# Weight sums of three square products made early and kept in DRAM, with three smaller edits, in a one-layer streaming encoder

## The chip, the core and the metric

The kernel runs on one core of a Trainium2 chip. The metric is the device time of one execution in microseconds (us). TensorE (PE) does the matmuls and loads their weights, VectorE (DVE), ScalarE (ACT) and GpSimd (POOL) do elementwise work, and the SyncE queue (SP) issues the DMAs, one after the other.

## What is computed

One layer over 1024 new frames of one stream and 64 frames of a running one, 1088 columns of width 1024 in all, in float32. The reference, cut to the parts that matter here:

```python
h = x + 0.5 * swiglu(rmsnorm(x, g_ffn1), w_ffn1_gu, w_ffn1_d)           # ffn1, D_FF = 2816
z = rmsnorm(h, g_mix) @ w_in                                            # projection: [u | q | k | v]
y_ssm = glu(s5(u));  y_att = diff_attn(q, k, v)                         # two head groups
h = h + concat(y_ssm, y_att) @ w_out                                    # square product "out", 1024 x 1024
mk, mv = rmsnorm(mem, g_mem) @ w_ck, rmsnorm(mem, g_mem) @ w_cv         # memory keys and values
q = rmsnorm(h, g_cross) @ w_cq                                          # square product "cq"
h = h + (softmax(q @ mk.T / 16) @ mv) @ w_co                            # square product "co"
y = rmsnorm(h + 0.5 * swiglu(rmsnorm(h, g_ffn2), ...), g_final)         # ffn2
```

## The kernel before

**Precision.** Every float32 operand is split in two parts of TensorE's reduced format, a high and a low part, and a product is three matmuls (hi·hi, hi·lo, lo·hi; `mm3`, L171, tiles 128 wide, mostly 272 columns). For a weight tile `split_into` (L147) makes the high part `wh` on ACT (L151), makes a second rounded copy `q` on ACT (L152), and subtracts on DVE (L153) to get the low part `wl`. `q` lies in PSUM in a pool that has one buffer, so the next split's copy waits until this subtraction has read it. `w_raw` loads a weight piece into one of four "wr" tiles, `half` gives one of four half-size "ws" tiles, `row` one of 36 rows; `wh` and `wl` have 7 buffers each.

**Squares.** The three 1024 x 1024 products are done as seven products of half size each, one per turn, in the order `TURNS = (0, 1, 3, 4, 5, 2, 6)`. Class `Block` loads the four quarters of a weight (`a11`, `a12`, `a21`, `a22`, four row blocks k each). `mix` (L433 to L435) makes three sums of quarters on POOL and `prepare` a fourth (L448), 16 POOL operations of 128x512 in all for a square. `prepare` also splits the weight (L446) and the data operand: L422 and L426 make the data's differences, L450 and L451 their high and low parts. `square` (L468) runs the turns: four output blocks i per turn, 24 matmuls each, then the additions to the outputs (L502); after each block the operand of the next turn is prepared.

**FFN.** Both FFNs use class `Operands`: `high` on ACT (L340), `low` (L345) on POOL for row blocks k in `LOW_G = (1, 3)` and on DVE for the others. POOL also makes the FFN's weight sums (L616 to L619) and its joins (L646, L647, L775).

**Memory.** `mem_proj` projects 256 memory rows, first with w_cv, then with w_ck (PE L1700, copies L1707), through `load_w`, which splits by `split_into`.

**Norm sums.** `Normed.finish` multiplies squared sums by a 128-wide matrix of ones (L543), five column tiles into two banks of PSUM, and copies a column of each out (L545, L547).

**Order.** The source appends generators to a background list `bg` and pumps them, but the final order on every engine is laid out by a scheduler that simulates the program; it may put an operation well ahead of its place in the source. SP issues the DMAs in one row, so a DMA that waits holds back those behind it. The stages from the span's start, in us: ffn1 to 752 (its last down block from 696), norm to 803, projection with the S5 scans 805 to 1030, GLU and attention to 1210, memory values to 1240, out to 1340, memory keys 1340 to 1382, cq to 1474, cross attention to 1540, co to 1643, norm, ffn2 to the end.

## Time and profile before

| | us |
|---|---|
| median of 3 runs (2411.47 to 2418.18) | 2415.66 |
| the profiled execution | 2410.96 |
| its span | 2409.2 |
| PE busy (94% of the span) | 2267.8 |
| DVE busy (68%) | 1646.8 |
| ACT busy (54%) | 1308.8 |
| POOL busy (46%) | 1102.1 |
| mean granted TensorE clock, of 1 | 0.978 |

The time is the span and what lies around it, 1.8 us here. PE is busy nearly throughout, so the time can fall by what PE idles in, by what it works through at a lower granted clock, or by less work for it. A granted clock of 1 is 2.4 GHz and of 0.5 is 1.2 GHz; a stretch of T us with a mean clock c has lost about T x (1 - c) if PE had work all through.

### The profile page before, as it was taken

What the parts mean: (1) busy time and instruction counts of PE and PEld (TensorE: products, weight loads), DVE (VectorE), ACT (ScalarE), POOL (GpSimd) and SP (SyncE); (2) the same over time, 40 slices, a digit from 0 to 9 for tenths busy, and PEclk for the clock granted to TensorE, in tenths of its full rate; (3) what the DMA queues carried; (4) which work ended last, traced back from release to release, by engine and by line L of the source; (5) the groups of instructions that cost most, each with busy time, mean ns of one, the idle gap of its engine ahead of it and who ended that gap; (6) DMA issues with size and microseconds to landing.
All of it is one profiled execution on the core that took longest, in us unless ns stands there. A gap on an engine that the chain in (4) does not pass through costs nothing. (4 is left out here: it accounts for less than half of the span.)

```text
span 2409.2 us, 44963 instructions
## 1 busy us (share of the span) xinstructions
PE 2267.8 (94%) x16914; PEld 2199.7 (91%) x16914; DVE 1646.8 (68%) x3296; ACT 1308.8 (54%) x2538; POOL 1102.1 (46%) x846
## 2 busy tenths in 40 slices
PE   6899999999999999989999899898899999998998
PEld 6899999998999998978889898798899999998997
DVE  6557543358899594269968688787654454479897
ACT  6554544546545422267856667576555544464543
POOL 2666777744144400035444510455776666644350
PEclk8999999999999999999999999999999999999999
DMA  6232444443412446333443411133232222262312
GB/s 207 75 114 82 118 110 118 117 174 141 145 42 82 155 126 171 93 128 105 134 156 111 164 50 53 54 116 94 83 97 81 78 70 77 81 227 82 110 47 93
DMA packets 267237, 262.61 MB, mean 109 GB/s; under 512 B 36446, under 2 KB 216715, under 8 KB 267019
## 3 DMA queue, kind: packets, MB, share of 16 engines
q1 hardware_dynamic: 266928, 259.72, 33.7%
q8 instruction: 133, 2.18, 0.4%
q14 instruction: 86, 0.70, 0.1%
q10 hardware_dynamic: 90, 0.02, 0.0%
HBM read 186.51 MB, written 68.58 MB: 106 GB/s over the span
## 5 line engine op out<-in xcount | busy, mean ns | idle before, releaser
L171 PE MATMUL b<-r,wh 128*128 128x272 f32 (+4 forms) x9600 | 1684.7, 296 | 54.1 <-DVE r L724 21.5
L171 PEld LDWEIGHTS b<-r,wh 128*128 128x128 f32 x9600 | 1420.1, 191 | 72.3 <-DVE r L724 26.2
L171 PE MATMUL b<-r,wl 128*128 128x272 f32 (+4 forms) x4800 | 1053.1, 295 | 25.4 <-DVE wl L153 25.2
L171 PEld LDWEIGHTS b<-r,wl 128*128 128x128 f32 x4800 | 782.7, 190 | 29.6 <-DVE wl L153 29.4
L596 DVE TENSOR_TENSOR r<-b,r 128x272 f32<-128x272 f32 x440 | 172.1, 434 | 247.1 <-PE b L171 227.7
L153 DVE TENSOR_TENSOR wl<-wr,q 128x512 fp32r<-128x512 f32 x304 | 207.2, 682 | 182.0 <-issue 94.6
L151 ACT CAST wh<-wr 128x512 fp32r<-128x512 f32 x304 | 187.7, 621 | 252.0 <-PE b L171 226.4
L152 ACT CAST q<-wr 128x512 fp32r<-128x512 f32 x304 | 179.9, 592 | 246.7 <-DVE wl L153 244.5
L451 DVE TENSOR_TENSOR r<-r,r 128x544 fp32r<-128x544 f32 x224 | 213.0, 968 | 24.1 <-ACT r L450 22.9
L433 POOL TENSOR_TENSOR ws<-r,r 128x512 f32<-128x512 f32 x32 | 53.2, 1670 | 307.9 <-DVE ws L1826 125.2
L153 DVE TENSOR_TENSOR wl<-ws,q 128x512 fp32r<-128x512 f32 x158 | 107.7, 681 | 96.2 <-PE b L171 53.4
L151 ACT CAST wh<-ws 128x512 fp32r<-128x512 f32 x158 | 98.0, 620 | 137.3 <-PE b L171 112.1
L152 ACT CAST q<-r 128x512 fp32r<-128x512 f32 x146 | 86.3, 591 | 125.5 <-DVE wl L153 125.3
L450 ACT CAST r<-r 128x544 fp32r<-128x544 f32 x224 | 143.5, 649 | 8.8 <-DMA r<-hid_d 7.2
L724 DVE SCALAR_TENSOR_TENSOR r<-b,r 128x272 f32<-128x272 f32 (+4 forms) x328 | 132.3, 438 | 22.7 <-PE b L171 21.7
L152 ACT CAST q<-ws 128x512 fp32r<-128x512 f32 x158 | 93.8, 594 | 87.4 <-DVE wl L153 80.2
L646 POOL TENSOR_TENSOR r<-r,r 128x544 f32<-128x544 f32 x44 | 61.5, 1398 | 169.8 <-DVE r L596 133.1
L153 DVE TENSOR_TENSOR wl<-r,q 128x512 fp32r<-128x512 f32 x146 | 99.5, 681 | 36.9 <-ACT q L152 35.8
L1425 POOL CAST r<-r 64x256 fp32r<-64x256 f32 x32 | 14.5, 454 | 237.2 <-ACT r L1342 221.5
L659 POOL TENSOR_TENSOR r<-r,r 128x1088 f32<-128x1088 f32 x44 | 112.0, 2548 | 8.8 <-ACT r L658 8.8
L151 ACT CAST wh<-r 128x512 fp32r<-128x512 f32 x146 | 90.0, 620 | 42.4 <-PE b L171 28.1
L137 PE MATMUL b<-ident,r 128*128 128x128 f32 (+4 forms) x649 | 92.3, 280 | 18.4 <-DMA r<-x_prompt 9.6
(343 smaller groups left out, 2965.4 us busy)
## 6 DMA issues: line engine op xcount, KB each, us to landing
wr<-w_ffn_gu SPq DMA_DIRECT2D x194, 256.0 KB, 2.9
hid_d<-r SPq DMA_DIRECT2D x44, 544.0 KB, 3.1
r<-hid_d SPq DMA_DIRECT2D x44, 544.0 KB, 6.6
h_d<-r SPq DMA_DIRECT2D x48, 272.0 KB, 2.5
r<-h_d SPq DMA_DIRECT2D x48, 272.0 KB, 2.8
r<-w_ffn_d SPq DMA_DIRECT2D x24, 512.0 KB, 7.0
wr<-w_in SPq DMA_DIRECT2D x32, 256.0 KB, 2.6
wr<-w_ffn_d SPq DMA_DIRECT2D x20, 256.0 KB, 2.8
```

Source lines behind the costliest of these rows:

```text
L137: T.transpose(out, in_, ident[:n, :n])
L151: A.copy(hi, x)
L152: A.copy(r, x)
L153: V.tensor_tensor(out=lo, in0=x, in1=r.bitcast(F32), op=ALU.subtract)
L171: T.matmul(pc[:, :c1 - c0], w, x[:, c0:c1], start=(first + i == 0 and q == 0), stop=(first + i == n - 1 and q == 2))
L433: G.tensor_tensor(out=s1, in0=a21, in1=a22, op=ALU.add)
L450: A.copy(r[:, 0], v)
L451: V.tensor_tensor(out=r[:, 1], in0=v, in1=r[:, 0].bitcast(F32), op=ALU.subtract)
L596: V.tensor_tensor(out=oc, in0=pc, in1=tc_, op=ALU.add)
L646: G.tensor_tensor(out=gate[:, T2], in0=gate[:, T2], in1=up[:, T2], op=ALU.add)
L659: G.tensor_tensor(out=up, in0=up, in1=gate, op=ALU.mult)
L724: V.scalar_tensor_tensor(out=hc_, in0=pc, scalar=0.5, in1=hc_, op0=ALU.mult, op1=ALU.add)
```

## The change

1. `LOW_G` becomes empty: `low` of every row block goes to DVE.
2. `w_split` gets a flag. In `mem_proj` the copy `q` is left out, and the low part is the raw tile minus `wh`, both in SBUF.
3. A generator `weight_sums` makes the four sums for a weight ahead of its square and stores them in `sums_d` in DRAM: for each k it loads 8 pieces of 128x2x128 into the four "ws" tiles, runs 16 POOL operations of 128x128, and stores four tiles. That is 32 loads, 64 POOL operations and 16 stores for a weight. In the source, w_out's generator stands before the projection's first unit, those of w_co and then w_cq before its third key unit. `SquareBlock` takes `Block`'s place: it loads the right quarter or sum for each turn from DRAM (28 loads of 256 KB for a square) and has no POOL work. The tiles for turns 0, 3 and 6 are "ws" tiles, those for 1 and 4 "wr" tiles, the rest rows.
4. `Normed.finish` multiplies by four columns of ones in place of 128 and uses one bank.

```diff
-LOW_G = 1, 3
+LOW_G = ()
...
-    def w_split(raw):
+    def w_split(raw, staged=True):
...
+        if staged:
+            split_into(hi, lo, raw)
+        else:
+            A.copy(hi, raw)
+            V.tensor_tensor(out=lo, in0=raw, in1=hi.bitcast(F32), op=ALU.subtract)
...
+    def weight_sums(n, w, swap=False):
+        i11, i21, i12, i22 = (1, 0, 3, 2) if swap else (0, 1, 2, 3)
+        for k in range(4):
+            ts = [half([P, 4, P]) for _ in range(4)]
+            for c, t in enumerate(ts):
+                for h in range(2):
+                    wj = w[(4 * h + k) * P:(4 * h + k + 1) * P].rearrange("p (h c n) -> p h c n", h=2, c=4)
+                    load(out=t[:, 2 * h:2 * h + 2], in_=wj[:, :, c])
+            yield
+            for c, t in enumerate(ts):
+                a11, a21, a12, a22 = (t[:, i] for i in (i11, i21, i12, i22))
+                G.tensor_tensor(out=a22, in0=a21, in1=a22, op=ALU.add)
+                G.tensor_tensor(out=a21, in0=a11, in1=a21, op=ALU.subtract)
+                G.tensor_tensor(out=a11, in0=a22, in1=a11, op=ALU.subtract)
+                G.tensor_tensor(out=a12, in0=a12, in1=a11, op=ALU.subtract)
+                store(out=sums_d[n, k, c], in_=t)
+    class SquareBlock(Block):
...
+        def fetch(self, n, k):
+            if n >= 7:
+                return
+            q, g = TURNS[n], n % 3
+            if g < 2:
+                t = self.held("wr" if g else "ws", k, (lambda: wp.tile([P, 512], F32, tag="wr", name=nm("wr"), bufs=4))
+                              if g else lambda: half([P, 512]))
+            else:
+                t = self.held("w2", k // 2, lambda: row([P, 2, 512]))[:, k % 2]
+            if q in (0, 1, 5):
+                j, h = (k if q == 0 else 4 + k), (q == 5) != self.swap
+                load(out=t, in_=self.wd[j * P:(j + 1) * P, 512 * h:512 * h + 512])
+            else:
+                i = {2: 3, 3: 0, 4: 1, 6: 2}[q] ^ self.swap
+                load(out=t.rearrange("p (c n) -> p c n", c=4),
+                     in_=sums_d[self.number, k, :, :, i].rearrange("c p n -> p c n"))
+            self.raw[q, k] = t
+        def prepare(self, q, k, late=False):
...
+            self.w[q, k] = self.held.split_w(self.raw[q, k])
+            self.operand(q, k, late)
...
-            p, q = bank(), bank()
+            p = bank()
             for t, (t0, n) in enumerate(HTILES):
...
+                T.matmul(p[:n, 4 * t:4 * t + 4], self.acc[:, c, t0:t0 + n], ones[:, 0:4], start=True, stop=True)
...
+    bg.append(weight_sums(0, a["w_out"][0]))
     for f in range(4):
...
+        if hd == SUMS_AT:
+            bg.append(chain(weight_sums(2, a["w_co"][0]), weight_sums(1, a["w_cq"][0], True)))
...
-                wk = load_w(wv[:, :, c * P:(c + 1) * P])
+                wk = load_w(wv[:, :, c * P:(c + 1) * P], False)
...
-    d = Block(Held(), 4, weights_of(a["w_out"][0]), cat)
+    d = SquareBlock(0, a["w_out"][0], cat)
```

Where the scheduler puts the moved work shows in the engines' orders. First POOL at the start of ffn1's last down block (about 696 us in the trace of before), before the change; `r` are rows, L775 the down block's joins:

```order
L448 TENSOR_TENSOR r_7333<-r_7333,wr_7244 128x512
L775 TENSOR_TENSOR r_6898<-r_6898,r_6798 128x544
L775 TENSOR_TENSOR r_6900<-r_6900,r_6800 128x544
L775 TENSOR_TENSOR r_6902<-r_6902,r_6802 128x544
L775 TENSOR_TENSOR r_6904<-r_6904,r_6804 128x544
L775 TENSOR_TENSOR r_6988<-r_6988,r_6798 128x544
```

The same place after the change; L831 is the old L775, L482 to L485 are the sums of w_out in "ws" tiles:

```order
L448 TENSOR_TENSOR r_7334<-r_7334,wr_7245 128x512
L482 TENSOR_TENSOR ws_9788<-ws_9788 128x128
L483 TENSOR_TENSOR ws_9788<-ws_9788 128x128
L831 TENSOR_TENSOR r_6899<-r_6899,r_6799 128x544
L484 TENSOR_TENSOR ws_9788<-ws_9788 128x128
L485 TENSOR_TENSOR ws_9788<-ws_9788 128x128
L482 TENSOR_TENSOR ws_9789<-ws_9789 128x128
L831 TENSOR_TENSOR r_6901<-r_6901,r_6801 128x544
```

All 64 sums of w_out stand here, among the joins of the last down block, ahead of the projection; those of w_co begin behind the projection's first scans and run on into its key units, and those of w_cq follow.

Next DVE at the start of co (about 1540 us), before the change; L1866 copies the last attention output, `wl` is a low part of a weight:

```order
L451 TENSOR_TENSOR r_18299<-r_17645,r_18299 128x544
L451 TENSOR_TENSOR r_18308<-r_17662,r_18308 128x544
L422 TENSOR_TENSOR r_17645<-r_17645 128x544
L451 TENSOR_TENSOR r_18317<-r_17870,r_18317 128x544
L1866 COPY r_18254<-b_18346 128x64
L1866 COPY r_18271<-b_18346 128x64
L422 TENSOR_TENSOR r_17662<-r_17662 128x544
L451 TENSOR_TENSOR r_18326<-r_17887,r_18326 128x544
L426 TENSOR_TENSOR r_17645<-r_18095,r_17645 128x544 x2
L422 TENSOR_TENSOR r_17870<-r_17870 128x544
L426 TENSOR_TENSOR r_17662<-r_18112,r_17662 128x544 x2
L422 TENSOR_TENSOR r_17887<-r_17887 128x544
```

After the change, from the last four of the corresponding rows on (L154 is the old L153):

```order
L422 TENSOR_TENSOR r_18179<-r_18179 128x544
L426 TENSOR_TENSOR r_17971<-r_18421,r_17971 128x544 x2
L154 TENSOR_TENSOR wl_18597<-ws_18588,q_18598 128x512
L422 TENSOR_TENSOR r_18196<-r_18196 128x544
L426 TENSOR_TENSOR r_18179<-r_18563,r_18179 128x544 x2
L426 TENSOR_TENSOR r_18196<-r_18580,r_18196 128x544 x2
L154 TENSOR_TENSOR wl_18606<-ws_18590,q_18607 128x512
L154 TENSOR_TENSOR wl_18615<-ws_18592,q_18616 128x512
L154 TENSOR_TENSOR wl_18624<-ws_18594,q_18625 128x512
L154 TENSOR_TENSOR wl_18689<-wr_18632,q_18690 128x512
```

The four low parts of turn 0 stand behind the data's differences now; before the change they were made before the first of these rows, during the cross attention.

Last DVE in the memory keys' projection (about 1350 us), before the change:

```order
L153 TENSOR_TENSOR wl_16098<-wr_16095,q_16099 128x512
L451 TENSOR_TENSOR r_16286<-r_14307,r_16286 128x544
L451 TENSOR_TENSOR r_16295<-r_14308,r_16295 128x544
L422 TENSOR_TENSOR r_14307<-r_14307 128x544
L451 TENSOR_TENSOR r_16304<-r_14309,r_16304 128x544
L422 TENSOR_TENSOR r_14308<-r_14308 128x544
L451 TENSOR_TENSOR r_16313<-r_14310,r_16313 128x544
L426 TENSOR_TENSOR r_14307<-r_14311,r_14307 128x544
L153 TENSOR_TENSOR wl_16133<-wr_16130,q_16134 128x512
```

After the change (L163 is the subtraction without `q`):

```order
L163 TENSOR_TENSOR wl_16464<-wr_16461,wh_16463 128x512
L163 TENSOR_TENSOR wl_16497<-wr_16494,wh_16496 128x512
L163 TENSOR_TENSOR wl_16503<-wr_16500,wh_16502 128x512
L1763 COPY r_16210<-b_16365 128x512
L1763 COPY r_16211<-b_16371 128x512
L154 TENSOR_TENSOR wl_16592<-ws_16583,q_16593 128x512
L455 TENSOR_TENSOR r_16597<-r_14692,r_16597 128x544
```

The keys' low parts have moved ahead of cq's data operands, which stood among them.

## Rows read from the trace of the kernel before

**Rows 1.** The page, part 1: busy us of each engine, share, instructions.
```profile
PE 2267.8 (94%) x16914; PEld 2199.7 (91%) x16914; DVE 1646.8 (68%) x3296; ACT 1308.8 (54%) x2538; POOL 1102.1 (46%) x846
```

**Rows 2.** Waits of PE (us, times, longest) at 85-110, 905-920, 1240-1290, 1338-1382, 1555-1590, 1640-1662.
```profile
PE b L171 <- POOL r L345: 4.8, 3, 2.7
...
PE b L1284 <- ACT r L1286: 5.0, 1, 5.0
...
PE b L171 <- DVE r L1707: 3.9, 1, 3.9
...
PE b L1700 <- DVE wl L153: 5.1, 4, 2.3
...
PE b L171 <- DVE wl L153: 10.5, 3, 8.5
...
PE b L543 <- DVE hq L545: 3.9, 1, 3.9
```

**Rows 3.** Windows: busy time of each engine in eight stretches, granted clock (PEclk), DMA.
```profile
core 0: us, PE busy (x) PEld busy (x) DVE busy (x) ACT busy (x) POOL busy (x), PEclk, DMA share, GB/s
...
60.00:120.00 60.00, 52.64 (x376) 50.69 (x375) 34.68 (x56) 30.36 (x59) 37.57 (x27) 0.91 0.26 77
...
720.00:760.00 40.00, 35.48 (x277) 34.60 (x276) 38.66 (x56) 19.19 (x34) 24.24 (x16) 1.00 0.18 58
...
865.00:925.00 60.00, 54.44 (x345) 53.23 (x344) 57.19 (x156) 14.01 (x25) 0.00 (x0) 0.91 0.49 138
...
1242.00:1340.00 98.00, 89.47 (x678) 88.11 (x677) 80.12 (x130) 64.90 (x119) 58.39 (x40) 0.97 0.37 126
1340.00:1382.00 42.00, 33.33 (x229) 30.11 (x228) 26.84 (x42) 24.91 (x49) 16.81 (x11) 0.88 0.54 173
...
1540.00:1643.00 103.00, 90.74 (x693) 88.87 (x693) 92.75 (x148) 70.79 (x130) 60.07 (x39) 0.95 0.26 86
1643.00:1660.00 17.00, 12.27 (x76) 11.31 (x76) 15.28 (x21) 13.67 (x27) 10.10 (x7) 0.82 0.34 106
...
1740.00:2125.00 385.00, 384.86 (x3066) 384.64 (x3065) 191.47 (x333) 192.60 (x347) 251.63 (x147) 1.00 0.27 87
```

**Rows 4.** Timelines of POOL and DVE, 88-108: start, us, operation, [idle before <-releaser].
```profile
97.71 1.34 POOL L345 TENSOR_TENSOR r<-r,r 128x544 fp32r<-128x544 f32 x1
...
99.75 1.17 DVE L345 TENSOR_TENSOR r<-r,r 128x544 fp32r<-128x544 f32 x1 [3.75 <-ACT r L340]
```

**Rows 5.** Timeline of DVE at the start of out and in the memory keys.
```profile
1243.20 6.36 DVE L426 TENSOR_TENSOR r<-r,r 128x544 f32<-128x544 f32 x4
...
1253.35 0.69 DVE L153 TENSOR_TENSOR wl<-r,q 128x512 fp32r<-128x512 f32 x1 [0.66 <-ACT q L152]
...
1369.06 6.14 DVE L426 TENSOR_TENSOR r<-r,r 128x544 f32<-128x544 f32 x4
```

**Rows 6.** Timelines of PE, DVE and POOL around the start of co.
```profile
1539.81 1.01 PE L171 MATMUL b<-r,wh 128*128 128x272 f32 x6
...
1538.10 2.75 DVE L451 TENSOR_TENSOR r<-r,r 128x544 fp32r<-128x544 f32 x2 [5.56 <-ACT r L450]
...
1556.38 1.81 DVE L451 TENSOR_TENSOR r<-r,r 128x544 fp32r<-128x544 f32 x1
...
1565.59 0.71 DVE L426 TENSOR_TENSOR r<-r,r 128x544 f32<-128x544 f32 x1
1566.22 0.71 DVE L451 TENSOR_TENSOR r<-r,r 128x544 fp32r<-128x544 f32 x1
...
1557.57 1.77 POOL L434 TENSOR_TENSOR r<-wr,r 128x512 f32<-128x512 f32 x1
```

**Rows 7.** POOL by line and form: 696-760 (first row), the whole span (others).
```profile
L775 POOL TENSOR_TENSOR r<-r,r 128x544 f32<-128x544 f32 x20 | 31.3, 1571 | 32.7 <-DVE r L724 23.0 <-DVE r L775 9.4
...
L1090 POOL TENSOR_TENSOR r<-r 128x448 f32<-128x448 f32 x16 | 18.6, 1160 | 1.5 <-DVE wl L153 1.0
...
L1090 POOL TENSOR_TENSOR r<-r 128x64 f32<-128x64 f32 x8 | 2.6, 331 | 0.0
```

More of the change, by code (lines that the diff above doesn't have):

```diff
@@ L34 @@
 NPAIR = 16
+SUMS_AT = 2
 S_CHS = ((0, 360), (360, 720), (720, 1088))
@@ L153, in split_into, with load_w @@
         V.tensor_tensor(out=lo, in0=x, in1=r.bitcast(F32), op=ALU.subtract)
-    def w_split(raw):
+    def w_split(raw, staged=True):
         hi = wp.tile([P, 4, P], F32R, tag="wh", name=nm("wh"))
         lo = wp.tile([P, 4, P], F32R, tag="wl", name=nm("wl"))
-        split_into(hi, lo, raw)
+        if staged:
[3 more added lines that the diff above has]
+            V.tensor_tensor(out=lo, in0=raw, in1=hi.bitcast(F32), op=ALU.subtract)
         return hi, lo
-    def load_w(src):
-        parts = [w_split(w_raw(src[:, k:k + 4])) for k in range(0, src.shape[1], 4)]
+    def load_w(src, staged=True):
+        parts = [w_split(w_raw(src[:, k:k + 4]), staged) for k in range(0, src.shape[1], 4)]
         return [(hi[:, k], lo[:, k]) for hi, lo in parts for k in range(4)]
@@ L403, in load @@
                 self.a21[k] = held("a21", k // 2, lambda: row([P, 2, 512]))[:, k % 2]
-                halves = (wj[:, 512:1024], wj[:, 0:512]) if self.swap else (wj[:, 0:512], wj[:, 512:1024])
-                load(out=self.a11[k], in_=halves[0])
-                load(out=self.a21[k], in_=halves[1])
+                load(out=self.a11[k], in_=wj[:, 0:512])
+                load(out=self.a21[k], in_=wj[:, 512:1024])
             else:
@@ L409, in load @@
                 self.a12[k], self.a22[k] = both[:, 0], both[:, 1]
-                if self.swap:
-                    for c in range(2):
-                        load(out=both[:, c], in_=wj[:, 512 - 512 * c:1024 - 512 * c])
-                else:
-                    load(out=both, in_=wj.rearrange("p (c m) -> p c m", c=2))
+                load(out=both, in_=wj.rearrange("p (c m) -> p c m", c=2))
         def value(self, q, k, late):
@@ L448, in prepare, with operand @@
                 G.tensor_tensor(out=w, in0=w, in1=self.a11[k], op=ALU.subtract)
+            self.operand(q, k, late)
+        def operand(self, q, k, late):
+            held = self.held
             v, r = self.value(q, k, late), held("x", 4 * (held.turn[1] % 2) + k, lambda: row([P, 2, HT], F32R))
@@ L462, in product, with __init__ @@
             return p
+    sums_d = dram([3, 4, 4, P, 4, P], "sums_d")
+    def weight_sums(n, w, swap=False):
[15 more added lines that the diff above has]
+    class SquareBlock(Block):
+        def __init__(self, number, w, u, swap=False):
+            super().__init__(Held(), 4, None, u, swap=swap)
+            self.number, self.wd, self.raw = number, w, {}
+        def fetch(self, n, k):
[16 more added lines that the diff above has]
+        def prepare(self, q, k, late=False):
+            if k == 0:
+                self.held.turn[1] += 1
+            self.w[q, k] = self.held.split_w(self.raw[q, k])
+            self.operand(q, k, late)
     TURNS = (0, 1, 3, 4, 5, 2, 6)
@@ L511, in square @@
                     d.prepare(TURNS[n + 1], i, True)
+                d.fetch(n + 3, i)
                 if n in (0, 2, 3, 4):
@@ L540, in finish @@
             V.memset(ssq, 1.0)
-            p, q = bank(), bank()
+            p = bank()
             for t, (t0, n) in enumerate(HTILES):
-                T.matmul((p if t < 4 else q)[:n, (t % 4) * P:(t % 4 + 1) * P], self.acc[:, c, t0:t0 + n], ones,
-                         start=True, stop=True)
-            V.tensor_copy(ssq[:, 0:4], p.rearrange("p (t n) -> p t n", n=P)[:, :, 0])
+                T.matmul(p[:n, 4 * t:4 * t + 4], self.acc[:, c, t0:t0 + n], ones[:, 0:4], start=True, stop=True)
             n = HT - 512
-            V.tensor_copy(ssq[:n, 4:5], q[:n, 0:1])
+            V.tensor_copy(ssq[:, 0:4], p[:, 0:16].rearrange("p (t n) -> p t n", n=4)[:, :, 0])
+            V.tensor_copy(ssq[:n, 4:5], p[:n, 16:17])
             if self.rb is None:
@@ L1669, in tile_hymba_step @@
                 bg.append(subln(heads[m // 8]))
-    def weights_of(w):
-        return lambda k: w[k * P:(k + 1) * P]
     def begin(d):
-        for k in range(4):
-            d.load(1, k)
-        for k in range(4):
-            d.prepare(0, k)
-        for k in range(4):
-            d.load(3, k)
+        for n in range(3):
+            for k in range(4):
+                d.fetch(n, k)
+            if n == 0:
+                for k in range(4):
+                    d.prepare(0, k)
     h2_d = dram([KT, P, NT], "h2_d")
@@ L1815, in tile_hymba_step @@
     bg.append(cache_prep())
-    d = Block(Held(), 4, weights_of(a["w_cq"][0]), h2, swap=True)
+    d = SquareBlock(1, a["w_cq"][0], h2, swap=True)
     begin(d)
@@ L1879, in tile_hymba_step @@
         c_values(*q.popleft())
-    d = Block(Held(), 4, weights_of(a["w_co"][0]), oc)
+    d = SquareBlock(2, a["w_co"][0], oc)
     begin(d)
```

## The prediction, made before the changed kernel ran

> **What bounds the kernel now.** I read the engines' busy times first: PE is busy for 2267.8 of 2409.2 us [rows 1], so some 141 us of idle time, and what passes at half clock, are all that this change can touch, since it takes only six matmuls away. Next come the waits of PE in the stretches that the change names [rows 2], and the windows around them [rows 3]. From a window I take two losses: its length minus PE's busy time, and its length times one minus the granted clock, which is what work at the lower of the two levels (1.2 in place of 2.4 GHz) costs a PE that is busy. In 60-120 that is 7.4 + 5.4 us, in out (1242-1340) 8.5 + 2.9, in the memory keys (1340-1382) 8.7 + 5.0, in co (1540-1643) 12.3 + 5.2, in the norm behind it (1643-1660) 4.7 + 3.1: 63 us in all, the ceiling of the gain. What must not be overlooked is how close VectorE is to being a second bound: 38.7 of 40 us in 720-760 and 57.2 of 60 in 865-925.
>
> **LOW_G, start of ffn1.** PE waits 4.8 us there for three subtractions on POOL [rows 2]. Each takes 1.34 us itself and stands in a queue of weight sums and joins, while VectorE sits idle for 3.75 us ahead of its own subtraction of 1.17 us [rows 4]. Moved to VectorE (14 operations in the first 120 us, 34.7 of 60 us busy in 60-120 [rows 3]), they find room; POOL's queue shortens by as much. I take the 4.8 us and half of the clock's 5.4, minus 0.5 for subtractions that now queue behind each other: **7 us** (2 to 11). In co and the norm 8 more operations move to VectorE, at 0.63 us from start to start [rows 6], 5 us that its relief there (below) covers; without it they would cost up to those 5 us, which the lower end for co takes in.
>
> **out.** Four operations of 128x544 took 6.36 us on VectorE at 1243 [rows 5], against 0.63 us for one when POOL is idle [rows 6]: 3.8 us lost while POOL mixed weights. The copies for PE stand behind them, and PE waits 3.9 us for those [rows 2]. Without mixing that wait goes; of the other 4.6 us of idle time I count half, and of the clock's 2.9 us the same share (6.2 of 8.5): 3.9 + 2.3 + 2.1 = **8 us** (2 to 11). The 28 loads from DRAM have a whole turn or more of lead and are hidden; if they were not, each square would stall where a turn begins.
>
> **Memory keys.** Two things go. A split can start only every 1.35 us, since its copy `q` waits for the one buffer (0.69 us of subtraction and the 0.66 us of idle time in front of it [rows 5]); 16 splits take 21.6 us of a stretch of 42. Without `q` a subtraction of some 0.69 us sets the pace. And four operations took 6.14 us in place of 2.5 while POOL mixed w_cq [rows 5]; the order shows cq's operands behind the keys' low parts now. Of 8.7 us of idle time I count 6, 5.1 of it the waits for `wl` [rows 2], and the same share of the clock's 5.0, 3.4: **9 us** (4 to 13). In the memory values the PE is not kept waiting, and cq loses little as it is: nothing for either (0 to 2).
>
> **co.** From about 1554 to 1565 VectorE and POOL took turns, one operation each per 1.74 us (1.81 and 1.77 us long), where VectorE alone starts one every 0.63 us [rows 6]: seven operations took 10.9 us instead of 4.4, and PE waited 10.5 us for the low parts behind them [rows 2]. That goes. But turn 0's weights now sit in "ws" tiles, which cross attention holds almost until co's first matmul at 1539.8 [rows 6]; its low parts, earlier made during the attention, now stand in VectorE's order behind eleven operations on data and two copies. From 1538.1 on [rows 6], at 0.63 us each, I place the first at 1546.1, the others at 1549.9, 1551.3 and 1552.6, the last three 1.35 us apart by the chain of `q` [rows 5]. PE has 14, 20 and 20 matmuls of 0.125 us (385 us by 3066 [rows 3]) between them, so it waits 4.6 and 1.3 us, and in turn 1, whose fourth low part comes at 1567.0 by the same count, 1.5 us. Old losses 10.5 and 5.2 (clock), new ones 7.4, and up to 5.2 again if the clock falls: a gain of 3.1 to 8.3, **5 us** (-3 to 10).
>
> **Norm.** A narrow product saves next to nothing itself; the one bank less removes the 3.9 us wait for the copy behind VectorE's row of differences [rows 2], unless the next product, which waits for a bank as well, inherits it. Of 7.8 us I take half, **4 us** (0 to 8).
>
> **What the sums cost.** No row shows a 128x128 sum on POOL. Between 331 ns at 128x64 and 1160 ns at 128x448 [rows 7] a straight line gives 0.47 us, 30 us for a weight's 64. By the order, w_out's sums stand in ffn1's last down block, where POOL is busy for 31.3 of 64 us [rows 7]: it fits, barely, with joins of 1.57 us queued behind sums and, on SP, loads of the next stage's rows and weights behind 16 stores that wait for them. VectorE has no slack there. It has about 35 all-SBUF operations, partly slowed by the joins already; if each waits out one sum in the remaining 60% of the time, 10 us. PE was idle for 4.5 of 40 us waiting for VectorE [rows 3], so delay passes on. Between 0 and 12 I take **5 us**. Some 32 sums of w_co fall into 868-920, where POOL was empty and VectorE is full with scans: 0 to 15 us (32 by 0.47) on top of the 5.0 us wait at 912 [rows 2], **5 us** since scans with a PSUM operand or a long running time absorb most. w_cq's sums run at 955-1020 beside idle engines. Each weight costs 4.2 MB read and 4.2 written for its sums, and 7.3 MB in place of 4.2 in its square, 34 MB in all; the DMA engines are busy for 0.18 to 0.54 of the stretches concerned [rows 3]: 0 (0 to 3).
>
> **Sum.** 7 + 8 + 9 + 5 + 4 = 33 us gained, 10 lost, 23 net. Against the profiled execution, 2410.96 us, that is 2388; it lies 4.7 us under the median of the runs shown, and against that median of 2415.66 I predict **2393 us**.
>
> **Rivals.** First, *VectorE and POOL exclude each other on every sum*. In co each operation of one waited out a whole one of the other [rows 6]. If each of the 64 + 32 sums that fall into full VectorE stretches cost it 0.47 us, the bill is 45 us against 33: +12, **2428 us**. This is also how the change fails to do what it says, since w_out's sums are not made in the projection, with its idle POOL, but 100 us earlier. It turns slower from 33/96 = 0.34 us per sum, measurably from 0.42; my 10 us are 0.10. Against it: low parts that read `q` in PSUM keep 0.69 us while POOL works [rows 5], and PSUM readers are a large part of the down block. The Trainium skill, "SBUF — State Buffer" (section "SBUF: two separate sides"), calls the port pair that the two share an exclusive lock, held for a whole instruction, which a VectorE operation with two SBUF inputs meets when a GpSimd operation reads SBUF; the lockstep in co agrees, and by that rule the sums hurt just where both are full, and the keys' new subtraction without `q` would be exposed as well, were POOL not empty there now.
>
> Second, *the waits move to the next in line*. A square needs 84 us of PE (672 matmuls of 0.125 us). VectorE was busy for 92.8 us in co [rows 3]; without the 6.5 us of lockstep 86 are left, as much as PE needs. If VectorE's own sum sets the squares' pace, the keys finish early only to wait for cq's data, and the norm passes its wait on, LOW_G's 7 us alone stay against 10 lost: +3, **2419 us**, no change. For it: these 86 us. Against it: the waits stand at a few places, where a queue of data differences bunches ahead of a low part, not in every turn; PE is idle for 12.3 of the 103 us, and 10.5 of these are one bunch [rows 2, 3].
>
> Third, *everything is had*: the upper ends, 11 + 11 + 13 + 10 + 8, with no cost: -53, **2363 us**. It needs POOL's small sums to slip between VectorE's operations everywhere.
>
> **How the numbers follow.** A chance of 0.60 for the forecast, 0.15 for the lock, 0.17 for moved waits, 0.08 for everything. About 0.3%, 7 us, is what a measurement of this kernel can tell from no change. The forecast's own spread (the ends above taken as independent, some 15 us either way) crosses into no change in one case of nine, and the third rival is faster: faster 0.61, within 0.3% 0.23, slower 0.16. The range takes in the moved waits, and below, most of the forecast's spread: 2370 to 2420.
>
> **What would show it.** LOW_G: no wait of PE for a POOL subtraction before 120 us. out and keys: four data differences in 2.5 us in place of 6.4, splits in the keys less than 1.35 us apart, both windows shorter by 8 and 9 us. co: PE waits of about 5 us near 1545 in the old count and none of 8 us behind. Sums: VectorE operations in the last down block over 1.2 us long next to 0.47 us sums, and the norm beginning some 5 us late. I would be wrong most easily in the costs: if the down block ends 15 us late, the first rival is right, and if the squares still take 98 to 103 us, the second.

## The result

The changed kernel takes 2397.0 us (2393.9 to 2401.6, 4 runs) against 2415.1 us (2411.5 to 2418.2): a ratio of 0.9927, 95% interval 0.9905 to 0.9949, 18 us faster. 2393 had been forecast. A second set of runs gave 2399.2 against 2416.4. The profiled execution is one of 2398.3 us, 12.7 us below that of before, which was a quick one of its kind.

Part 1 of the page of the changed kernel, which answers to [rows 1]: PE is busy for 5 us less than before and idle for some 8 us less, so the gain is idle time and time at half clock. Its number of instructions is the same, 16914: the change takes no matmul away, where the prediction has six.

```profile
PE 2262.8 (94%) x16914; PEld 2197.2 (92%) x16914; DVE 1644.8 (69%) x3318; ACT 1290.2 (54%) x2506; POOL 1101.7 (46%) x968
```

Where it went is read best from the start of the same matmul in both traces. The first group of an S5 output unit is at 956.13 before and at 973.99 after: +17.9 us. The transposes in cq are at 1439.74 and 1434.89: -4.9. Timelines of PE, first before (L1284, L137), then after (L1340, L138):

```profile
956.13 0.39 PE L1284 MATMUL b<-r,r 128*128 128x136 f32 x2
...
1439.74 0.60 PE L137 MATMUL b<-ident,r 128*128 128x128 f32 x4
```

```profile
973.99 0.39 PE L1340 MATMUL b<-r,r 128*128 128x136 f32 x2
...
1434.89 0.60 PE L138 MATMUL b<-ident,r 128*128 128x128 f32 x4
```

The table gives such differences of starts for eight landmarks and all runs, in us against the trace of before (negative is ahead). The landmarks, named by their time before: background work in ffn1 (291), the norm's sums (803), the S5 output (956), the end of the attention (1227), late cq (1440), the end of the cross attention (1536), the norm behind co (1645), the last transposes (2397). The last columns are the median of the runs and the ratio to before with its interval. Two executions of one kernel (after, after_again) differ by some 3 us already at 291.

| kernel | 291 | 803 | 956 | 1227 | 1440 | 1536 | 1645 | 2397 | median us | ratio |
|---|---|---|---|---|---|---|---|---|---|---|
| after | -4.4 | +4.1 | +17.9 | +19.2 | -4.9 | -6.7 | -9.3 | -12.8 | 2397.0 | 0.9927 (0.9905 to 0.9949) |
| after_again | -1.2 | +7.5 | +19.6 | +20.5 | -5.2 | -8.6 | -11.2 | -14.5 | 2399.2 | 0.9936 (0.9922 to 0.9949) |
| no_sums | -4.7 | -4.1 | -4.3 | -3.0 | -28.0 | -31.3 | -33.9 | -34.2 | 2378.5 | 0.9853 (0.9834 to 0.9872) |
| sums_dma_only | -5.0 | -2.8 | +1.6 | +11.5 | -14.1 | -16.1 | -18.2 | -22.0 | 2393.3 | 0.9912 (0.9890 to 0.9934) |
| sums_after_s5 | -4.7 | -4.6 | -4.2 | +34.1 | +10.4 | +7.0 | +4.9 | +4.5 | 2410.5 | 0.9982 (0.9971 to 0.9993) |
| sums_split | -2.9 | -2.4 | -2.5 | +16.9 | -2.6 | +4.2 | +1.8 | -1.9 | 2409.6 | 0.9972 (0.9961 to 0.9983) |
| sums_apart | -5.2 | +3.5 | +3.8 | +5.2 | -13.9 | -7.6 | -10.1 | -12.5 | 2401.4 | 0.9942 (0.9928 to 0.9957) |
| sums_gap | -5.8 | -2.5 | +10.6 | +10.1 | -12.4 | -6.5 | -8.5 | -4.7 | 2412.1 | 0.9985 (0.9975 to 0.9994) |
| after_staged | -2.1 | +7.1 | +22.8 | +25.3 | +9.7 | +7.8 | +5.8 | +2.0 | 2410.5 | 0.9974 (0.9965 to 0.9984) |
| squares_only | +1.7 | +11.1 | +22.6 | +24.2 | +8.4 | +6.6 | +1.2 | +6.8 | 2419.3 | 1.0013 (1.0002 to 1.0023) |
| lowg_only | -4.7 | -4.1 | -3.7 | -3.5 | -3.0 | -3.5 | +1.7 | +0.6 | 2411.7 | 0.9976 (0.9966 to 0.9985) |
| keys_only | +1.0 | +1.1 | +1.3 | +5.9 | +0.5 | -1.6 | -1.6 | -2.8 | 2411.8 | 0.9978 (0.9967 to 0.9988) |
| finish_only | -0.3 | -0.5 | -0.8 | -0.8 | +2.2 | +2.3 | +1.1 | +2.3 | 2415.4 | 0.9998 (0.9987 to 1.0009) |

So the change first wins 4 us, loses 8.5 in ffn1's last down block and 14 in the projection, and then wins 24 from the end of the attention to late cq. The windows after answer to [rows 3]; their bounds are moved to the same work (out and the first half of the keys 1259-1362, the rest of the keys and cq 1362-1435):

```profile
60.00:120.00 60.00, 55.60 (x422) 54.42 (x422) 41.88 (x69) 33.31 (x62) 30.40 (x20) 0.97 0.27 80
724.00:764.00 40.00, 32.99 (x231) 31.90 (x230) 36.65 (x47) 15.34 (x26) 38.66 (x39) 0.91 0.42 134
869.00:929.00 60.00, 52.40 (x317) 50.70 (x316) 59.93 (x145) 13.87 (x25) 26.68 (x31) 0.90 0.55 160
929.00:974.00 45.00, 39.52 (x240) 39.31 (x240) 14.32 (x27) 8.73 (x17) 14.56 (x30) 0.91 0.88 249
1259.00:1362.00 103.00, 99.62 (x781) 98.78 (x781) 82.00 (x139) 71.84 (x133) 40.14 (x26) 0.98 0.58 190
1362.00:1435.00 73.00, 73.00 (x589) 72.66 (x589) 60.45 (x115) 48.20 (x94) 0.00 (x0) 1.00 0.47 148
1530.00:1636.00 106.00, 96.68 (x725) 93.06 (x723) 91.11 (x158) 79.46 (x146) 34.74 (x24) 0.98 0.47 148
```

The columns are the length, then the busy time of PE, its weight loads, DVE, ACT and POOL, then clock, DMA share and GB/s. Read them from the PE column and the clock: 73.00 of 73.00 us at clock 1.00 in the keys and cq, where the keys alone had idled 8.7 of 42. In the down block PE idles 7 of 40 us at 0.91 where it had idled 4.5 at 1.00, with POOL at 38.7 of 40. In 869-929 VectorE is busy for 59.93 us with 145 operations, where it had done 156 in 57.19 us [rows 3]. And in 929-974 the DMA engines are busy at 0.88, PE waits for 5.5 us, and the clock falls.

### The profile page after: what moved, and what is told of

Read it like the earlier page. It is cut to its first block, busy times and chain, and to the rows that moved or that the text cites. A ratio compares the mean times of both kernels' runs of the same rounds, so it can differ in the third digit from the quotient of the medians.

```text
span 2396.5 us, 45406 instructions
## 1 busy us (share of the span) xinstructions
PE 2262.8 (94%) x16914; PEld 2197.2 (92%) x16914; DVE 1644.8 (69%) x3318; ACT 1290.2 (54%) x2506; POOL 1101.7 (46%) x968
## 5 line engine op out<-in xcount | busy, mean ns | idle before, releaser
L154 DVE TENSOR_TENSOR wl<-wr,q 128x512 fp32r<-128x512 f32 x272 | 185.4, 682 | 150.0 <-issue 77.9
L153 ACT CAST q<-wr 128x512 fp32r<-128x512 f32 x272 | 161.4, 593 | 229.7 <-DVE wl L154 221.0
L152 ACT CAST wh<-wr 128x512 fp32r<-128x512 f32 x272 | 167.9, 622 | 196.8 <-PE b L176 191.4
L455 DVE TENSOR_TENSOR r<-r,r 128x544 fp32r<-128x544 f32 x224 | 201.4, 919 | 22.9 <-ACT r L454 22.4
L154 DVE TENSOR_TENSOR wl<-ws,q 128x512 fp32r<-128x512 f32 x182 | 123.9, 681 | 100.3 <-PE b L176 53.7
L152 ACT CAST wh<-ws 128x512 fp32r<-128x512 f32 x182 | 112.7, 620 | 137.6 <-PE b L176 110.0
L593 POOL TENSOR_TENSOR r<-r,r 128x544 f32<-128x544 f32 x28 | 43.6, 1558 | 282.2 <-ACT r L592 281.5
L153 ACT CAST q<-ws 128x512 fp32r<-128x512 f32 x182 | 107.8, 592 | 113.4 <-DVE wl L154 98.2
L153 ACT CAST q<-r 128x512 fp32r<-128x512 f32 x122 | 72.4, 593 | 126.4 <-DVE wl L154 126.3
L702 POOL TENSOR_TENSOR r<-r,r 128x544 f32<-128x544 f32 x44 | 62.4, 1419 | 161.3 <-DVE r L652 135.8
L672 POOL TENSOR_TENSOR ws<-wr,wr 128x512 f32<-128x512 f32 x44 | 60.4, 1372 | 156.9 <-DMA wr<-w_ffn_gu 126.4
L138 PE MATMUL b<-ident,r 128*128 128x128 f32 (+4 forms) x649 | 92.5, 280 | 23.9 <-DMA r<-x_prompt 10.6
L138 PEld LDWEIGHTS b<-ident,r 128*128 128x128 f32 (+4 forms) x649 | 74.6, 144 | 34.9 <-DMA r<-x_prompt 10.6
L154 DVE TENSOR_TENSOR wl<-r,q 128x512 fp32r<-128x512 f32 x122 | 83.1, 681 | 29.3 <-ACT q L153 25.0
```

The lines of the kernel that those rows point to most:

```text
L138: T.transpose(out, in_, ident[:n, :n])
L152: A.copy(hi, x)
L153: A.copy(r, x)
L154: V.tensor_tensor(out=lo, in0=x, in1=r.bitcast(F32), op=ALU.subtract)
L455: V.tensor_tensor(out=r[:, 1], in0=v, in1=r[:, 0].bitcast(F32), op=ALU.subtract)
L672: G.tensor_tensor(out=s1, in0=r[2], in1=r[3], op=ALU.add)
```

## How the projection loses 14 us

It loses them in two steps. Up to the matmul that stood at 908 before, the offset goes from +4.2 to +8.3 (from +7.5 to +10.7 in after_again). PE stands for 1.9 us in front of a transpose, for a copy of the projection (L203) that comes behind the scans on VectorE, and the clock falls with it (0.83 in 900-910). VectorE is busy all through there, and its operations beside POOL's sums are longer; twelve equal scan operations took 249 ns each before (L1206) and take 336 ns after (L1262). Waits of PE, 890-912, after; then VectorE by line and form, 865-935, before and after:

```profile
PE b L138 <- DVE r L203: 1.9, 1, 1.9
```

```profile
L1206 DVE TENSOR_TENSOR r<-ws,r 128x64 f32<-128x64 f32 x12 | 3.0, 249 | 0.0
```

```profile
L1262 DVE TENSOR_TENSOR r<-ws,r 128x64 f32<-128x64 f32 x12 | 4.0, 336 | 0.0
```

The second step, 9 us, lies near 945. The queue SP before, then SP, VectorE, ACT and PE after (timelines; L1289 and L1345 store an S5 output in ys_d, L486 stores sums, PE L1340 is an S5 output, DVE L1263 a scan step, ACT L1398 the copy of transposed attention rows that frees the bank for PE):

```profile
912.33 3.19 SPq L1289 DMA_DIRECT2D ys_d<-r  x7
...
921.65 0.42 SPq L1289 DMA_DIRECT2D ys_d<-r  x1
```

```profile
926.24 0.33 SPq L486 DMA_DIRECT2D sums_d<-ws  x1
...
927.15 3.43 SPq L1345 DMA_DIRECT2D ys_d<-r  x7
...
937.28 0.42 SPq L1345 DMA_DIRECT2D ys_d<-r  x1
```

```profile
942.71 0.96 DVE L1263 TENSOR_TENSOR r<-ws,apn 128x476 f32<-128x476 f32 x1 [6.73 <-DMA ws<-w_co]
```

```profile
947.30 1.07 ACT L1398 COPY r<-b 128x512 f32<-128x512 f32 x2 [10.17 <-DVE r L1322]
```

```profile
947.94 0.82 PE L1340 MATMUL b<-r,r 128*128 128x136 f32 x2 [5.48 <-DMA ws<-w_co]
```

VectorE stands for 6.7 us in the middle of a scan step. By its semaphores that step waits for the eight stores of an S5 output that last used its row, in both kernels, and the last of the eight is issued 9 to 10 us after the first in both. (The profile names ws<-w_co, a transfer that reuses one of these semaphores.) What differs is when the first store is issued. Before, ACT has made the last piece of that output at 912.3, and the store follows at once. After, the piece is there at 920.6, 8.3 us later, like PE; but the store is issued at 927.15, since SP stands until then in front of loads and stores of sums. When the scan step and the sum behind it (L1322) are done, ACT copies, at 947.30, and PE goes on as the first copy ends, at 947.94.

The transfers themselves are not what makes it late. The DMA engines are busy at 84% here, against 60% before, but the 512 KB load that SP issues just ahead of the last store takes 5.2 us to land, and one next to it took 5.1 before (transfers, 925-945, after, then 909-929, before: the queue's packets, MB and share; issues, KB each, median us to landing):

```profile
q1 hardware_dynamic: 6844, 4.66, 84.2%
...
r<-rk_d SPq DMA_DIRECT2D x1, 512.0 KB, 5.2
```

```profile
q1 hardware_dynamic: 4698, 3.24, 59.9%
...
r<-m_d SPq DMA_DIRECT2D x1, 512.0 KB, 5.1
```

SP's own waits in 860-960, after. It stands 14.6 us in front of stores of sums until POOL has made them, and in front of the next tiles' loads 10.0 us until the stores have landed and 8.9 us until VectorE is through with a scan operation; all that follows on SP stands with it.

```profile
SPq L486 <- POOL ws L485: 14.6, 5, 5.2
SPq L478 <- DMA sums_d<-ws: 10.0, 5, 3.0
SPq L478 <- DVE r L1264: 8.9, 3, 7.9
```

## Experiments

**The sums away, and their transfers alone.** no_sums drops the two appended generators and loads a raw quarter for every turn; sums_dma_only drops the four POOL operations.

```diff
-    bg.append(weight_sums(0, a["w_out"][0]))
...
-            bg.append(chain(weight_sums(2, a["w_co"][0]), weight_sums(1, a["w_cq"][0], True)))
...
-            if q in (0, 1, 5):
+            if True:
```

> Leaves out the making of the weight sums: no loads, POOL operations or stores for them, and the squares load raw quarters in place of the sums, from the same DRAM loads' number and size. In the trace after the change the kernel is 4.0 us ahead of before at 480 us, 4.2 us behind at 830 us, and 17.9 us behind at 960 us. If all of that 22 us is the price of the sums, wherever it comes from, this kernel is some 22 us faster than the changed one, about 2375 us, with the projection 4 us ahead of before throughout. If part of it comes from the new order alone (tiles, loads of the squares), it stays above 2385.

```diff
-                G.tensor_tensor(out=a22, in0=a21, in1=a22, op=ALU.add)
-                G.tensor_tensor(out=a21, in0=a11, in1=a21, op=ALU.subtract)
-                G.tensor_tensor(out=a11, in0=a22, in1=a11, op=ALU.subtract)
-                G.tensor_tensor(out=a12, in0=a12, in1=a11, op=ALU.subtract)
```

> Leaves out the 192 POOL operations of the sums and keeps their loads and stores. Queue theory (the sums' transfers on SP and the DMA engines hold up the scans' own transfers): VectorE's wait of 6.7 us and PE's of 5.5 us near 945 us stay, the projection still loses 8 to 14 us, and the kernel lands at 2385 to 2392. Port theory (POOL's sums slow VectorE's operations on SBUF): both losses go, the down block's 8 us and the projection's 14, and it lands at about 2375, as without any sums.

Without sums: 2378.5 us, and the offset stays at -4 through the whole projection. Making the sums costs 19 to 21 us, against 2397.0 and 2399.2. With the transfers alone it is 2393.3: 15 us for the transfers, and 4 to 6 more for the POOL operations, which the intervals do not separate. The offsets say where. The transfers cost 2.2 us up to 803 (with POOL's operations it is 8.5), and 14.3 between 803 and 1227, as much as transfers and POOL operations together do in the changed kernel (15.1). But they cost it at another place. Up to 956 they cost 4.4 of the changed kernel's 13.8; its first step is missing, and of PE's 5.5 us near 945, which the queue theory expected to stay, 1.8 are left (with 2.2 more for a load, r<-rk_d). Of the other 10, 8 are lost near 1000: sums that POOL no longer slows move up there, and ACT waits for weights of the projection, whose loads stand behind them on SP. So the two prices do not add up from parts: what POOL's operations cost the stretch up to 956, some 9 us, is VectorE's longer operations and SP's standing for POOL. Waits of PE, no_sums in 860-960, then of ACT and PE, sums_dma_only in 985-1015:

```profile
PE b L1340 <- ACT r L1342: 4.9, 1, 4.9
```

```profile
ACT wh L152 <- DMA wr<-w_in: 29.4, 2, 22.3
...
PE b L176 <- ACT r L1394: 3.4, 1, 3.4
```

The 4.9 us are the wait of [rows 2] at 912, which is the same in all three kernels (5.1 in the changed one).

**All sums behind S5.** A one-column POOL copy of the last S5 state into the first tiles orders them; one chain makes all three.

```diff
+    bg.append(chain(weight_sums(0, a["w_out"][0], after=s_fin), weight_sums(1, a["w_cq"][0], True), weight_sums(2, a["w_co"][0])))
...
+            if after is not None and k == 0:
+                for t in ts:
+                    G.tensor_copy(t[:, 0, 0:1], after[:, 1, 1, NPAIR - 1:NPAIR])
```

> Same work as the changed kernel, but all three weights' sums start after the last S5 state is made (a one-column POOL copy of that state into the first tiles orders them), so they run in the projection's last units and the attention. Both theories of the cost expect the down block's 8 us back; the queue theory also the wait near 945 us, since the scans' transfers are then ahead: 2373 to 2382. If traffic and POOL work in the attention, where PE already waits for POOL at a few places, cost as much as they did before: 2390 to 2400.

Both theories of the expectation missed: 2410.5 us. Up to 1030 the sums now cost nothing, down block and projection included (-4.2 at 956). Then 38 us go at two places. Waits of PE in 1025-1090, and of ACT in 1015-1040:

```profile
PE b L1504 <- POOL r L1468: 24.3, 2, 22.6
PE b L176 <- ACT r L209: 10.0, 1, 10.0
```

```profile
ACT wh L162 <- DMA wr<-w_cv: 15.0, 1, 15.0
```

The first head's key rows (L1468) stand on POOL behind sums, which run on until 1110, and on ACT the GLU's operands (L209) stand behind a weight of the memory values whose load stands on SP behind sums. It is the queues again, three of them this time.

**Sums split up.** sums_split puts w_out's and w_cq's behind S5, and w_co's in four sets into the squares, at turns 0 and 3 of out and cq.

```diff
+    bg.append(chain(weight_sums(0, a["w_out"][0], after=s_fin), weight_sums(1, a["w_cq"][0], True)))
+    co_sums = weight_sums(2, a["w_co"][0])
...
+    def co_set(n, i):
+        if n in (0, 3) and i == 0:
+            next(co_sums)
+            next(co_sums)
```

> Same work as the changed kernel. The sums of w_out and w_cq start after the last S5 state (in the run with all three there they cost PE nothing up to 1030 us and were done by 1024), and those of w_co are made in four sets inside the squares out and cq, where POOL has little to do now. Queue theory: nothing is queued ahead of a transfer that PE needs soon, so the whole 18 to 22 us of the sums come back but for 0 to 6 us of slowed VectorE operations in the squares: 2375 to 2385. Port theory: 64 sums beside VectorE operations on SBUF in two squares, where VectorE is nearly the bound, cost what w_out's cost in the down block, 8 us or more: 2385 to 2392.

2409.6 us, above both expectations. PE waits 17.9 us for the GLU's operands: ACT stands 22.4 us at the copy `q` for out's turn 0, whose tile is one of the four "ws" tiles that w_cq's sums hold until about 1041. The expectation had these sums done by 1024; in sums_after_s5 only 112 of the 128 were, by 1029. Waits of PE in 1025-1050, timeline of ACT:

```profile
PE b L176 <- ACT r L209: 17.9, 1, 17.9
```

```profile
1042.62 0.59 ACT L153 CAST q<-ws 128x512 fp32r<-128x512 f32 x1 [22.39 <-DMA ws<-w_out]
```

sums_apart leaves w_out's in the down block and only w_cq's behind S5; sums_gap does the same and also holds w_out's until a power table of the scans is done; in its trace the copies that hold them run at 807, not at 817.

```diff
     bg.append(weight_sums(0, a["w_out"][0]))
...
+    bg.append(weight_sums(1, a["w_cq"][0], True, after=s_fin[:, 1, 1, NPAIR - 1:NPAIR]))
+    co_sums = weight_sums(2, a["w_co"][0])
```

> Same work as the changed kernel. w_out's sums stay in the last down block, w_cq's start after the last S5 state and w_co's are made in four sets in the squares out and cq. With all sums of w_out and w_cq behind S5, PE waited 17.9 us at 1046 for ACT, whose order holds a copy for out's first turn that waits for ws tiles; with w_cq's alone behind S5 the tiles come free by about 990, so that wait should be gone. Queue theory: the down block's 8 us stay, the projection's 14 are gone, the squares cost 0 to 4: 2381 to 2389. If what cost time there was POOL and DMA work as such, wherever it is put: 2393 to 2400.

```diff
-    bg.append(weight_sums(0, a["w_out"][0]))
+    bg.append(weight_sums(0, a["w_out"][0], after=wide[2][:, 0, 0:1]))
```

> As the one before, but w_out's sums wait for the last of the scan's power tables (about 817 us), so that they run beside the projection's first units, where POOL is idle and VectorE is busy for 38 of 60 us. If the down block's loss comes from POOL's sums between joins, its 6 to 8 us come back: 2375 to 2383. If SP then holds the scans' loads and the weights of the projection behind sums, PE or the scans wait there and it is no better than the one before: 2385 to 2395.

sums_apart, 2401.4 us, is no better than the changed kernel (2399.2 in the same runs; the intervals overlap). The projection is free as expected (+3.5 to +3.8). But from 1227 to 1440 it wins 19.1 us (19.5 in sums_split, 22.5 in sums_gap) where the changed kernel won 24 to 26, so w_co's sums in the squares cost 2 to 7 us. And from 1440 to 1536 these three lose 6 to 7 where the other variants of the changed kernel win 2 to 3: in sums_apart PE waits 5.0 us for a tile that VectorE scales in the cross attention, and ACT 13.6 us for the memory values' rows (r<-mv_d), which SP loads. sums_gap, 2412.1 us, also above both expectations, loses 12 us between 826 and 830: PE waits for the S5 input (r<-u_d), whose eight loads, issued in one row from 814 before, come at 815, 824 and 829, with transfers of the sums between them. It loses 7.5 more at the start of ffn2, in the same wait as squares_only (below). The waits: sums_apart, PE in 1455-1470 and ACT in 1440-1470, then sums_gap, PE in 815-845.

```profile
PE b L138 <- DVE ws L1894: 5.0, 4, 3.2
```

```profile
ACT r L209 <- DMA r<-mv_d: 13.6, 2, 13.2
```

```profile
PE b L1296 <- DMA r<-u_d: 9.3, 1, 9.3
```

**The parts one by one.** lowg_only, keys_only and finish_only make one small edit each on the kernel before; squares_only undoes all three in the changed kernel; after_staged undoes the memory edit alone.

```diff
-LOW_G = 1, 3
+LOW_G = ()
```

> The kernel before with LOW_G empty and nothing else. In four traces of variants of the changed kernel ffn1 runs 2 to 5 us ahead of before, where 7 had been forecast, since PE now waits for ACT at the same places. Alone it should give 4 to 5 us until 300 us and then hold it, and perhaps lose or gain 1 to 3 us at the start of ffn2 and in co, where 8 operations move to VectorE: 2409 to 2414.

Waits of PE, 85-110 and 1555-1662: POOL is gone from the first ([rows 2] had 4.8 us), and ACT has taken its place with 2.5 us (2.5 in the changed kernel, too). In co the 8.5 us wait is there as before, and one of 2.6 us for the outputs' additions has grown.

```profile
PE b L171 <- ACT r L340: 2.5, 2, 2.2
...
PE b L171 <- DVE wl L153: 11.2, 4, 8.5
PE b L543 <- DVE hq L545: 4.0, 1, 4.0
PE b L171 <- DVE r L502: 2.9, 2, 2.6
```

4.5 us in the median. Its trace wins 4.7 in ffn1 and loses 5.2 between 1536 and 1645: the 8 subtractions moved to VectorE cost there what was feared for the case without relief.

```diff
-                wk = load_w(wv[:, :, c * P:(c + 1) * P])
+                wk = load_w(wv[:, :, c * P:(c + 1) * P], False)
```

> The kernel before with the copy q of the memory projections left out and nothing else. If the one-buffer chain made the keys' waits, 1338 to 1382 becomes 5 to 9 us shorter: 2407 to 2411. If it needs the mixing out of the way as well (the subtraction now reads two SBUF operands and meets POOL's mixing of w_cq), 0 to 3 us: 2412 to 2416.

4.5 us in the median. The keys' waits for low parts go, and two waits for data operands come instead, in out at 1275 and in cq at 1392. POOL's mixing still slows VectorE there: from 1260 to 1274 POOL's operations take 1.74 to 1.77 us each and VectorE's data differences 1.2 to 1.8. From 1227 to 1440 the trace wins 5.4 us; between 956 and 1227 it loses 4.6 (waits of PE, 1240-1300 and 1370-1400):

```profile
PE b L175 <- DVE r L455: 6.3, 1, 6.3
```

```profile
PE b L175 <- DVE r L455: 3.2, 1, 3.2
```

```diff
-            p, q = bank(), bank()
+            p = bank()
```

> The kernel before with the narrow norm sums alone. In the changed kernel a wait of 2.9 us for the same copy stands where 3.9 and 0.8 us stood. If the bank was what PE waited for, the stretch 1643 to 1660 is 2 to 4 us shorter: 2411 to 2414. If the wait only moves to the next product, no change: 2415 to 2417.

No change (interval -0.13% to +0.09%). The wait of 3.9 us has moved from the norm's product to the next one, L171 in place of L543 (waits of PE, 1640-1662):

```profile
PE b L171 <- DVE hq L546: 3.9, 1, 3.9
```

> The changed kernel with the copy q of the memory projections put back. From 1240 to 1440 us the changed kernel gained 24 us over before. If the one-buffer chain of q made the keys' waits, some 6 to 9 us come back: 2403 to 2406, with waits of PE for low parts in the keys again. If POOL's mixing beside VectorE made them, which is gone either way, it stays within 2 us: 2395 to 2399.

The edit here is keys_only's, backwards. 2410.5 us, above both expectations: in the changed kernel the memory edit is worth 11.3 us (against after_again), not 4.5. From 1227 to 1440 the trace wins 15.6 us where the changed kernel wins 24 to 26, so 8.5 to 10 of it lie there, and the keys' waits are back (waits of PE, 1360-1395):

```profile
PE b L1756 <- ACT wh L152: 2.9, 3, 2.1
PE b L1756 <- DVE wl L154: 2.3, 2, 1.9
```

> The changed kernel without LOW_G, without the memory projections' edit and without the narrow norm sums: the sums and the squares alone, on the kernel before. Alone on before LOW_G gave 4.5 us and the memory edit 4.5, the norm nothing; the changed kernel is 18 to 19 us faster than before. If the parts add up, the squares alone are worth 9 to 10 us: about 2406. But the changed kernel without the memory edit lost 13.5 us instead of 4.5; if that is so because the edit is worth more once POOL is out of the way, the squares alone give nothing: 2413 to 2418.

Its edit is the change without the three small parts. 2419.3 us: sums and squares alone are worth nothing, and by the interval 0.5 to 5.6 us too slow. Alone, the four parts come to 4.5 + 4.5 + 0.9 - 2.9 = 7 us; together they gave 17 to 18. A large part of that gap is one wait that none of the arguments here covers. At the start of ffn2 squares_only loses 8.2 us (the offset goes from +1.3 to +9.6 at 1684): PE waits for the high part of a weight sum that POOL makes late. Its loads are issued on SP at 1677.6; in the changed kernel, where that part of ACT's wait is 3.4 us, they are issued at 1658.5. sums_gap has the same wait, 5.3 us, and none of the other traces has it at more than 1.6. Waits of PE, 1655-1700, and of ACT, 1650-1695:

```profile
PE b L176 <- ACT wh L152: 5.5, 1, 5.5
```

```profile
ACT wh L152 <- POOL r L673: 9.5, 1, 9.5
```

Without these 8 us the parts would come to 15, near the whole. What the traces do show of parts that need each other is the stretch from 1227 to 1440: there the memory edit wins 5.4 us on the kernel before, where VectorE hands some of it back at the next data operands beside POOL's mixing, and 8.5 to 10 in the changed kernel.

> The changed kernel once more, on the chip of these runs, so that the variants are compared on the same chip: 2394 to 2400.

2399.2 us, as expected; it was timed in one set with sums_apart, sums_gap and squares_only.

## Why the prediction held, point by point

It held in sum, 23 us forecast and 17 to 18 measured. That it came so close is in part luck, since two errors of opposite sign stand in it: without the cost of the sums the change gains 38 us (no_sums), not 33, and the sums cost 19 to 21, not 10.

**LOW_G, 7 us**: 4.5. The POOL waits went as described; what was overlooked is the next in line, ACT's high part, 2.5 us at the same matmuls.

**out 8, memory keys 9, cq 0**: 17 forecast, 24 measured in the changed kernel (from +19.2 to -4.9), 25.0 without sums. In squares_only, whose order there is that of before, the offset falls from +24.2 at 1227 to +14.0 at the keys' first product: out is 10. The keys and cq are then 14. Here the step "of 8.7 us of idle time I count 6" was too careful, since PE idles for nothing there now, and cq, put at nothing (0 to 2), had idled for 1.5 us before. Four data differences take 2.6 us at the start of out, near the 2.5 that the prediction gave as its sign. But "a subtraction of some 0.69 us sets the pace" holds only for half of the keys, and POOL was not empty there, as the prediction took it to be: the subtraction without `q` takes 0.69 us behind 1358, and 1.2 to 1.9 us in seven of the eight ahead of that, where POOL makes squares for the norm's sums; 1.10 on average (by line and form, 1259-1435):

```profile
L163 DVE TENSOR_TENSOR wl<-wr,wh 128x512 fp32r<-128x512 f32 x16 | 17.3, 1103 | 4.3 <-ACT wh L162 4.1
```

**co, 5**: 2.6 (from -6.7 to -9.3), and 5.4 in squares_only, without the eight LOW_G operations. Turn 0's new waits were worked out as 4.6, 1.3 and, in turn 1, 1.5 us, all after the first matmul; PE's waits at 1534 to 1568 were 0.9 (for a high part), 2.0, 0.9 and 1.3 (waits of PE, 1530-1600, after):

```profile
PE b L176 <- DVE wl L154: 5.5, 5, 2.0
```

The 8.5 us wait is gone and so is the lockstep. The relief does not fully cover LOW_G's operations, as the prediction had allowed.

**Norm, 4**: nothing alone. The clause "unless the next product, which waits for a bank as well, inherits it" was the truth of it. In the changed kernel a wait of 2.9 us is left, and of some 3 us that it wins at the norm (from -9.3 to -12.1 at 1660) half is gone again by 1676.

**What the sums cost, 10**: 19 to 21. This is the step that failed, and at one term. w_out's in the down block were put at 5 by VectorE waiting out sums; 8.5 were measured, of which POOL's operations make 6, or 0.1 us for each of the 64, as in the sum. How much of this is VectorE waiting out sums is not separated: some of its operations there are longer (below), and it also stands 3.4 us for a join that POOL makes late and 2.3 us for a load. w_co's in the S5 stretch were put at 5, again by VectorE beside POOL; 14 were measured, of which the first step, 4, is what that term meant. The other 9 to 10 lay in the sentence that counted traffic as 0 to 3 because the DMA engines were only half busy. That was a mean share; in the stretch they were at 0.6 before and are at 0.8 to 0.9 now, and yet the transfers land about as fast. What it left out is order: stores of sums wait for POOL and next loads wait for stores, on the one queue that also carries the scans' transfers and the projection's weights. With POOL's operations left out the 4 are gone, and the transfers cost 14 all the same, 10 of them by order at another place. The prediction had named loads behind 16 stores on SP, in the down block, and not in the stretch where SP carries the scan.

**The rivals.** *VectorE and POOL exclude each other on every sum* needed 0.34 us per sum; the down block shows 0.1, and the first step of the S5 stretch 4 us for some 32 sums, 0.13. *The waits move to the next in line* was wrong for the squares as a whole, 24 us didn't move, and right for the norm, for keys_only, and for LOW_G in co. *Everything is had* needed 53 us: no_sums, which leaves the whole cost of the sums out, is 38 below before, so the gains lie near the forecast's 33 and not at their upper ends. None of four other places for the sums did better than the changed kernel.

**What stays open.** Why SP issues ffn2's first loads so late in squares_only and sums_gap, why finish_only loses 1 us more behind 1645, and why keys_only loses 4.6 us between 956 and 1227 was not followed; these may come with the order that the scheduler lays out for each program. Whether the sums would be cheaper with their stores on another queue than SP was not tried.

## What to carry to other kernels

Before moving work to an idle engine, list every queue that its transfers join, and who else is on each: a store that waits for a slow engine stops all that follows on the same DMA queue, and an early operation of an in-order engine that waits for a shared tile stops all behind it. Price a moved step by that list, not by bandwidth or busy shares. And test the parts of a change together as well as alone, and look where a variant loses before adding up its parts: here four parts gave 7 us by themselves and 17 to 18 together, but 8 of the difference are one wait far from the change in one of the variants.

## What the hardware showed that was not expected

A 128x128 sum on POOL takes 0.46 us on average in 955-1020, where VectorE is mostly idle, near the 0.47 of the straight line, and 0.60 to 0.71 us on average in the last down block beside VectorE (POOL by line, 690-770, after: L483 and L484, with their idle time; the joins keep their 1.58 us):

```profile
L831 POOL TENSOR_TENSOR r<-r,r 128x544 f32<-128x544 f32 x20 | 31.4, 1578 | 0.0
L484 POOL TENSOR_TENSOR ws<-ws 128x128 f32<-128x128 f32 x16 | 11.3, 713 | 0.2
...
L483 POOL TENSOR_TENSOR ws<-ws 128x128 f32<-128x128 f32 x16 | 9.5, 602 | 0.2
```

The longest single sum that I looked at stands in the scans (timeline of POOL, 895-930, after):

```profile
898.87 3.31 POOL L482 TENSOR_TENSOR ws<-ws 128x128 f32<-128x128 f32 x1 [6.46 <-DMA ws<-w_co]
```

From 898.88 VectorE runs eight operations on SBUF operands without a pause; at 901.76 it comes to one that reads `q` in PSUM, and the sum ends at 902.18, 0.42 us later. It looks as if a short POOL operation can wait out several of VectorE's, where in co the two took turns [rows 6], and a store on SP that waits for the sum waits with it. One row does not prove it.

VectorE pays too, unevenly. In the down block its operations L455 hardly stretch (1.03 us on average, L451 before 1.01), while L426 goes from 1.00 to 1.50 and the joins on VectorE (L831) from 1.19 to 1.35 us (by line and form, 696-760, before, then after):

```profile
L426 DVE TENSOR_TENSOR r<-r,r 128x544 f32<-128x544 f32 x5 | 4.9, 1001 | 0.0
```

```profile
L426 DVE TENSOR_TENSOR r<-r,r 128x544 f32<-128x544 f32 x3 | 4.4, 1495 | 0.0
```

The Trainium skill, "SBUF — State Buffer" (section "SBUF: two separate sides"), states that of a VectorE operation with two SBUF inputs and a GpSimd operation that reads SBUF, the one that starts first holds their shared port for its whole instruction and the other blocks. The rows agree as far as one waits for the other; they do not show which one waits more often.
